# A two-layer trunk on one core: modulation scale on VectorE, low weight parts by adding transfers, one transfer rate in the planner, an earlier layer norm

## The chip, the core and the metric

The kernel runs on one core of a Trainium2 chip. A time is the device time of one execution in microseconds; the figure for a kernel is the median of several executions. The engines are named as in the profile: PE (TensorE, matmul) with PEld (its weight loads), DVE (VectorE), ACT (ScalarE), POOL (GpSimd) and SP (SyncE, whose queue carries most transfers).

## The reference: what is computed

Two layers run over 640 tokens (128 context tokens and 512 latent tokens) of width 1024. All is float32. Cut to what matters here:

```python
mod = silu(c) @ w_mod + b_mod              # six vectors a layer, for the context and for the latents
sh1, sc1, gt1, sh2, sc2, gt2 = split(mod, 6)
h = rmsnorm(x, g_pre_mix) * (1 + sc1) + sh1
bg, cg, xin, q, k, v, cf_u, ga, gb, gc = split_in(h @ w_in)      # 8704 columns
y_a = (bg * dwconv(cg * xin)) @ sc_w_out                         # width 3
y_b = diff_attention(q, k, v) @ attn_w_out                       # 8 heads, two maps each
z = dwconv(za * sigmoid(zg), cf_conv_w) + cf_conv_b              # width 31
y_c = silu(layernorm(z)) @ cf_w_out + cf_b_out
m = sigmoid(ga) * y_a + sigmoid(gb) * y_b + sigmoid(gc) * y_c
x = x + gt1 * rmsnorm(m @ w_o)
h = rmsnorm(x) * (1 + sc2) + sh2
x = x + gt2 * rmsnorm(square(relu(h @ w_ff1)) @ w_ff2)
```

## The kernel before

**Tiling.** Channels lie on the 128 partitions and the 640 tokens along the row, so x, h and every branch are 8 (or 4) tiles `u` of 128x640. A product is computed to nearly float32 with three fast matmuls: both operands are split into a high part, which the fast format holds exactly, and the rest. The tiles `h[k]` are such pairs.

**Weights.** `raw_load` brings a block of 128x1024 (512 KB) to one of three buffers `raw`, through SP's queue. `wblock` makes two of ten buffers `w` of it: `wh` is a cast on ACT, `wl = r - wh` a subtraction that the planner puts on DVE or on POOL (`nc.either`). A block serves 48 matmuls of 128x320. In the MLP `wseven` also knows another way to a low part for some of its seven operands: ACT writes `-r` to it (rounded as `wh` is), and a transfer issued from POOL reads the weight in memory again and adds it (`accum_op=ALU.add`).

**Order of the work.** The code is not issued as it is written. A `Recorder` collects operations with the tiles that they touch; `rank` gives each a due time (that of the matmul that needs it, less the durations on the way), and `schedule` plays the engines forward with modelled durations, picking what is due first, and sets each engine's order and what of `either` goes to POOL. In that model a transfer of SP's takes its bytes over 360 GB/s, one after another; a transfer of POOL's takes 3 us and its bytes over 150 GB/s, beside the others.

**Start.** The 8 tiles of x are loaded and squared, their mean square is summed over the channels on PE, and `rsb`, the reciprocal root for each token, is copied to all partitions. Then for each k of 8: x[k] is multiplied by `rsb`; the scale (j = 1) and the shift (j = 0) of block k are two products of a 128x1024 piece of `w_mod` with the two vectors `cc`: the piece comes as two tiles `u` of 128x512, and 8 matmuls with 2 columns (16 instructions in the profile, `ps<-cc,u`) give 2 columns of the PSUM tile `gp`, to which DVE adds the bias (`mod`). DVE makes `der` (gain times 1 + scale), ACT applies both (`u<-u,mod,der`), ACT and DVE split the result to `h[k]`, and `first_k` runs its matmuls: 12 of 128x256 (`pp<-u,w`) and 9 of 128x384 (`ps<-u,w`) for four blocks of `w_in`, the gates of the first two tiles of the long convolution; the fourth block's second part follows in `proj_half`. These are called the lead products here. All other modulation vectors are made later by `modvec`: a row-wise product of a raw tile with `cb` (c and c_ctx after silu, repeated on all partitions) and its sum on DVE, two of them for each tile (`junk<-raw,cb` and `raw<-raw,cb`). `cond` loads `cb`; it stands behind the lead loop.

**Attention part.** For each head `k_head` and `q_head` project, rotate (half of the rotation goes through 4 transfers `u<-u` inside SBUF) and split; `scores`, `softmax`, `values` and `v_pair` follow. `cgate` and `short` are the convolution branches; their taps run on DVE in between. `mt(i)` is a block of `w_in`.

**Gates.** `gated` runs three rounds of 8 tiles (A, B, C): the gate's product with h, a sigmoid, and the branch's product. `convnorm` is the layer norm of the long convolution in three steps (mean, variance, apply), one step with each of the tiles d = 5, 6, 7 of round A (`if d >= KD - 3: next(cn)`). Behind round A the heads' outputs `o` are loaded (`u<-on`, `u<-rqd`), scaled and split for round B.

Of the kernel before, what the change touches and what calls it, by code (L numbers as in the profile page):

```python
# [184 lines left out]


class Recorder:
# [132 lines left out]
    def rank(self):  # L320
# [18 lines left out]
        for op in reversed(self.ops):  # L339
            d = op.dur  # L340
            if op.eng == "sync":
                d = 1.3 + op.acts[1] / 360e3
            elif op.eng == "gpsimd" and op.acts is not None:
                d = 3.0 + op.acts[1] / 150e3
# [5 lines left out]
    def schedule(self):  # L350
# [91 lines left out]
        while len(seq) < n:  # L442
# [48 lines left out]
            if e == "sync":  # L491
                gen[0] = max(start, gen[0]) + 0.65
                dma[0] = max(gen[0] + 0.65, dma[0]) + op.acts[1] / 360e3
                op.end = dma[0]
            elif e == "gpsimd" and op.acts is not None:
                op.end = start + 3.0 + op.acts[1] / 150e3
            else:
                op.end = start + dur
# [34 lines left out]
def trunk_kernel(ctx: ExitStack, tc: tile.TileContext, xT, crow, ccol, wmod, wmod0, win, wv, wa, wc, wattn, wo, wff1, wff2,  # L533
# [68 lines left out]
    def wblock(src, eng=None):  # L602
# [3 lines left out]
        (eng or nc.either).tensor_sub(wl, r, f(wh))  # L606
# [288 lines left out]

    def modvec(l, st, j):
# [3 lines left out]
        for m in range(KD):  # L900
            r = raw_load(wmod[l, j * KD + m])
            for g in range(2):
                junk = r if g else wp.tile([P, KD * P], F32, tag="sum", name=nm("junk"), bufs=NSUM)
                nc.vector.tensor_tensor_reduce(out=junk, in0=r, in1=cb[:, g], op0=ALU.mult, op1=ALU.add, scale=1.0,
                                               scalar=0.0, accum_out=part[:, m, g:g + 1])
# [27 lines left out]
    nc.scalar.activation(cc, cc, AF.Silu)  # L933
    rsb = U()
# [5 lines left out]
    gp = PS()  # L940
    ts = [PP() for _ in range(2)]
# [9 lines left out]
    for k in range(KD):  # L951
        nc.either.tensor_mul(x[k], x[k], rsb)
        for j in (1, 0):
            i0 = j * KD + k
            r = half_tiles(wmod0[i0])
            sl = mod[:, i0, :]
            o = OFF["b_mod"][0] + i0
            nc.begin()
            for i in range(KD):
                c = (i % 4) * P  # L960
                nc.tensor.matmul(gp[:, 2 * i0:2 * i0 + 2], r[i // 4][:, c:c + P], cc[:, i, :], start=(i == 0),
                                 stop=(i == KD - 1))
            nc.done()
            nc.vector.tensor_scalar(sl, gp[:, 2 * i0:2 * i0 + 2], p[:, o:o + 1], None, op0=ALU.add)
# [9 lines left out]
    cond()  # L974
# [3 lines left out]
    for l in range(DEPTH):  # L978
# [3 lines left out]
        def mt(i):  # L982
            return wblock(win[l, i])
# [71 lines left out]
        def v_pair(pi):  # L1055
            wbs = [wblock(wv[l, 2 * pi + i]) for i in range(2)]
# [55 lines left out]
        def k_head(hd):  # L1112
# [3 lines left out]
            r = rope(proj2(wblock(win[l, W_K + hd]), h), kk, 1.0)  # L1116
# [9 lines left out]
        def q_head(hd):  # L1126

            r = rope(proj2(wblock(win[l, W_Q + hd]), h), None, QK ** -0.5)
# [186 lines left out]
        def gated(gate, n):  # L1315

            q = []
            for d in range(KD + n):
                if d < KD:
                    pg = proj(mt(gate + d), h)  # L1320
# [48 lines left out]
        for d, sg in gated(W_GA, 1):  # L1369
# [4 lines left out]
            if d >= KD - 3:  # L1374
# [245 lines left out]
def _layout(inp):  # L1620
# [8 lines left out]
    out["wmod0"] = _blocks(w0)  # L1629
# [71 lines left out]
```

## Time and profile before

| | |
|---|---|
| median of 3 runs (lowest, highest) | 2597.32 us (2591.19, 2600.37) |
| profiled execution: time, span | 2599.19 us, 2597.4 us |
| mean granted clock of TensorE | 0.972 |
| busy: PE, DVE, ACT, POOL | 96%, 74%, 48%, 11% |
| moved by the transfers | 336.76 MB, 130 GB/s over the span |

The profiled execution's time is 1.9 us above the median. Nearly all instructions carry one line of the code, that of the recorder's call, so groups are told apart by the names of the tiles: `out<-in`. The profile's rows of a timeline give start, duration, engine, operation, names, size and count, and in brackets the idle time before and what ended it. A table of windows gives the busy time of each engine in a stretch, the count of instructions, TensorE's granted clock as a share of full speed, the share of the transfer engines that was busy, and GB/s.

### The profile page before, as it was taken

What the parts mean: (1) busy time and instruction counts of PE and PEld (TensorE: products, weight loads), DVE (VectorE), ACT (ScalarE), POOL (GpSimd) and SP (SyncE); (2) the same over time, 40 slices, a digit from 0 to 9 for tenths busy, and PEclk for the clock granted to TensorE, in tenths of its full rate; (3) what the DMA queues carried; (4) which work ended last, traced back from release to release, by engine and by line L of the source; (5) the groups of instructions that cost most, each with busy time, mean ns of one, the idle gap of its engine ahead of it and who ended that gap; (6) DMA issues with size and microseconds to landing.
All of it is one profiled execution on the core that took longest, in us unless ns stands there. A gap on an engine that the chain in (4) does not pass through costs nothing.

```text
span 2597.4 us, 42157 instructions
## 1 busy us (share of the span) xinstructions
PE 2488.8 (96%) x16596; PEld 2412.5 (93%) x16596; DVE 1911.8 (74%) x3104; ACT 1250.4 (48%) x2323; POOL 290.7 (11%) x227
## 2 busy tenths in 40 slices
PE   7999999999999999999999999999999999999998
PEld 7988889999999899998988888999999999999998
DVE  3289786977785698878566887969566748677874
ACT  3365564223223566765445655532232247667653
POOL 1022110001020100012011211000011100001121
PEclk8899999999999999999989999999999999999999
DMA  7122222235554344577523222213454532447671
GB/s 269 48 93 65 66 68 71 87 127 194 176 178 138 99 166 175 191 176 187 171 87 97 76 62 77 73 56 115 154 174 137 175 110 96 140 156 210 176 216 56
DMA packets 132875, 336.76 MB, mean 130 GB/s; under 512 B 16244, under 2 KB 39108, under 8 KB 132676
## 3 DMA queue, kind: packets, MB, share of 16 engines
q1 hardware_dynamic: 122308, 315.19, 36.5%
q0 software_dynamic: 10368, 18.88, 4.3%
q8 instruction: 130, 2.13, 0.3%
q14 instruction: 69, 0.57, 0.1%
HBM read 284.15 MB, written 41.46 MB: 125 GB/s over the span
## 4 chain that ended last, share of the span: by engine, by line
PE 77%; DVE 11%; DMA 5%; ACT 4%; issue 2%; SPq 1%; POOL 0%; DVEq 0%; ACTq 0%; POOLq 0%
PE ps L529 41%; PE pp L529 35%; DVE u L529 8%; ACT u L529 3%; DMA raw<-in_wff_dram 2%; DMA u<-fd 2%; DVE w L529 1%; ACT w L529 1%; DVE mx L529 1%; DMA u<-u 1%; DVE sum L529 1%; SPq L529 1%; DMA u<-on 0%; DMA u<-rqd 0%; POOL st L529 0%
## 5 line engine op out<-in xcount | busy, mean ns | idle before, releaser
L529 PE MATMUL pp<-u,w 128*128 128x320 f32 (+1 forms) x6912 | 1069.6, 312 | 26.3 <-DVE u L529 12.9
L529 PE MATMUL ps<-u,w 128*128 128x320 f32 (+2 forms) x6672 | 1066.2, 315 | 12.1 <-DVE u L529 6.9
L529 PEld LDWEIGHTS pp<-u,w 128*128 128x128 f32 x6912 | 1030.1, 191 | 35.4 <-ACT u L529 13.6
L529 PEld LDWEIGHTS ps<-u,w 128*128 128x128 f32 x6672 | 1010.0, 191 | 25.0 <-DVE u L529 9.2
L529 ACT CAST w<-raw 128x1024 fp32r<-128x1024 f32 (+1 forms) x364 | 313.7, 863 | 290.2 <-PE ps L529 154.6
L529 DVE TENSOR_TENSOR w<-raw,w 128x1024 fp32r<-128x1024 f32 (+1 forms) x271 | 302.6, 1118 | 170.1 <-ACT w L529 166.7
L529 DVE TENSOR_TENSOR u<-u,u 128x640 fp32r<-128x640 f32 (+8 forms) x443 | 324.3, 744 | 72.8 <-ACT u L529 68.4
L529 ACT CAST u<-u 128x640 fp32r<-128x640 f32 (+2 forms) x280 | 195.5, 703 | 156.2 <-DVE u L529 79.7
L529 DVE SCALAR_TENSOR_TENSOR u<-u,par,u 128x640 f32<-128x640 f32 (+13 forms) x272 | 225.8, 863 | 1.7
L529 ACT ACTIVATE u<-u 128x320 f32<-128x320 f32 (+3 forms) x232 | 138.6, 612 | 117.8 <-DVE u L529 109.3
L529 DVE TENSOR_TENSOR w<-sum,w 128x512 fp32r<-128x512 f32 x208 | 143.4, 697 | 43.2 <-ACT w L529 42.2
L529 ACT CAST w<-sum 128x512 fp32r<-128x512 f32 x208 | 127.2, 621 | 87.2 <-PE pp L529 36.5
L529 ACT ACTIVATE u<-pp 128x640 f32<-128x640 f32 (+4 forms) x96 | 52.1, 552 | 234.1 <-PE pp L529 223.3
L529 POOL TENSOR_TENSOR u<-u,u 128x640 f32<-128x640 f32 (+4 forms) x60 | 104.6, 1747 | 503.2 <-DVE u L529 302.1
L529 DVE TENSOR_TENSOR u<-u,ps 128x320 f32<-128x320 f32 (+4 forms) x230 | 106.7, 481 | 52.8 <-PE ps L529 52.2
L529 DVE TENSOR_TENSOR u<-ps,u 128x512 fp32r<-128x512 f32 (+6 forms) x206 | 98.3, 505 | 59.8 <-PE ps L529 33.9
L529 DVE CUSTOM_DVE_ANT_0 junk<-raw,cb 128x1024 f32<-128x1024 f32 x80 | 102.5, 1283 | 46.7 <-DMA raw<-in_wmod_dram 46.5
L529 POOL DMA_DIRECT2D w<-in_wff_dram x72 | 62.9, 873 | 612.9 <-DVE sum L529 361.6
L529 PE MATMUL ps<-w,u 128*128 128x256 f32 x960 | 127.7, 291 | 2.8 <-ACT vo L529 2.8
L529 ACT ACTIVATE u<-pp,mx 128x640 f32<-128x640 f32 x128 | 101.0, 793 | 58.4 <-DVE mx L529 57.4
L529 PEld LDWEIGHTS ps<-w,u 128*128 128x128 f32 x960 | 120.9, 197 | 6.9 <-ACT vo L529 4.0
L529 POOL TENSOR_TENSOR w<-raw,w 128x1024 fp32r<-128x1024 f32 x21 | 52.9, 2521 | 565.6 <-ACT w L529 459.9
(90 smaller groups left out, 1874.5 us busy)
## 6 DMA issues: line engine op xcount, KB each, us to landing
raw<-in_wff_dram SPq DMA_DIRECT2D x128, 512.0 KB, 3.9
raw<-in_win_dram SPq DMA_DIRECT2D x120, 512.0 KB, 3.3
raw<-in_wmod_dram SPq DMA_DIRECT2D x80, 512.0 KB, 3.4
fd<-u SPq DMA_DIRECT2D x64, 320.0 KB, 2.4
u<-fd SPq DMA_DIRECT2D x64, 320.0 KB, 5.6
w<-in_wff_dram POOLq DMA_DIRECT2D x72, 256.0 KB, 5.8
u<-in_wmod_dram SPq DMA_DIRECT2D x32, 256.0 KB, 6.1
raw<-in_wv_dram SPq DMA_DIRECT2D x16, 512.0 KB, 3.3
```

What stands on the lines that cost most here:

```text
L529: getattr(eng, m)(*[r(v) for v in a], **{x: r(v) for x, v in k.items()})
```

## The change

1. **First scale on VectorE.** In the lead loop the shift (j = 0) stays on PE. The scale (j = 1) is made like the later modulation vectors: its piece of `w_mod` comes whole and with output channels on the partitions as a `raw` tile, two row-wise products with `cb` on DVE give `part[:, k]`, and DVE adds the bias. `cond` moves ahead of the loop.
2. **Low parts by adding transfers.** The blocks of `w_in` and of v's weights that pass through `mt` outside the gates, `v_pair`, `k_head` and `q_head` (40 a layer) get `wl` as in `wseven`: ACT writes `-r`, a POOL transfer adds the weight. The lead blocks and the gates' blocks keep the subtraction.
3. **Planner.** Transfers of SP and POOL share one modelled rate of 330 GB/s, an adding transfer counts twice its bytes, 0.7 to 1 us are added for landing, and the due times allow twice that duration.
4. **Layer norm one tile earlier.** `convnorm` takes its steps with d = 4, 5, 6.

```diff
+DMA = 330e3
...
             if op.eng == "sync":
-                d = 1.3 + op.acts[1] / 360e3
+                d = 2.0 + op.acts[1] / DMA / 0.5
             elif op.eng == "gpsimd" and op.acts is not None:
-                d = 3.0 + op.acts[1] / 150e3
+                d = 3.0 + 2 * op.acts[1] / DMA / 0.5
...
-                dma[0] = max(gen[0] + 0.65, dma[0]) + op.acts[1] / 360e3
-                op.end = dma[0]
+                dma[0] = max(gen[0] + 0.65, dma[0]) + op.acts[1] / DMA
+                op.end = dma[0] + 0.7
             elif e == "gpsimd" and op.acts is not None:
-                op.end = start + 3.0 + op.acts[1] / 150e3
+                dma[0] = max(start + 1.5, dma[0]) + 2 * op.acts[1] / DMA
+                op.end = dma[0] + 1.0
...
-    def wblock(src, eng=None):
+    def wblock(src, add=False):
         r = raw_load(src)
         wh, wl = wtile(), wtile()
         nc.scalar.copy(wh, r)
-        (eng or nc.either).tensor_sub(wl, r, f(wh))
+        if add:
+            nc.scalar.mul(wl, r, -1.0)
+            nc.gpsimd.dma_start(wl, src, accum_op=ALU.add)
+        else:
+            nc.either.tensor_sub(wl, r, f(wh))
         return wh, wl
...
+    def dots(r, out):
+        for g in range(2):
+            junk = r if g else wp.tile([P, KD * P], F32, tag="sum", name=nm("junk"), bufs=NSUM)
+            nc.vector.tensor_tensor_reduce(out=junk, in0=r, in1=cb[:, g], op0=ALU.mult, op1=ALU.add, scale=1.0,
+                                           scalar=0.0, accum_out=out[:, g:g + 1])
...
+    cond()
     rsb = U()
...
         for j in (1, 0):
             i0 = j * KD + k
-            r = half_tiles(wmod0[i0])
...
+            if j == 0:
+                r = half_tiles(wmod0[i0])
...
+            else:
+                r = raw_load(wmod0[i0])
+                dots(r, part[:, k])
+                nc.vector.tensor_scalar(sl, part[:, k], p[:, o:o + 1], None, op0=ALU.add)
...
-    cond()
...
         def mt(i):
-            return wblock(win[l, i])
+            return wblock(win[l, i], True)
...
-            wbs = [wblock(wv[l, 2 * pi + i]) for i in range(2)]
+            wbs = [wblock(wv[l, 2 * pi + i], True) for i in range(2)]
...
-            r = rope(proj2(wblock(win[l, W_K + hd]), h), kk, 1.0)
+            r = rope(proj2(wblock(win[l, W_K + hd], True), h), kk, 1.0)
...
-            r = rope(proj2(wblock(win[l, W_Q + hd]), h), None, QK ** -0.5)
+            r = rope(proj2(wblock(win[l, W_Q + hd], True), h), None, QK ** -0.5)
...
-                    pg = proj(mt(gate + d), h)
+                    pg = proj(wblock(win[l, gate + d]), h)
...
-            if d >= KD - 3:
+            if KD - 4 <= d < KD - 4 + 3:
                 next(cn)
...
-    out["wmod0"] = _blocks(w0)
+    out["wmod0"] = np.concatenate([_blocks(w0[:, :D]), w0[:, D:].T.reshape(KD, P, D)])
```

**What moves, engine by engine.** PE in the lead loop, before: the third block pair of k = 2 (`u_421` and `u_423` are `h[2]`, `ps_236` is `gp`, `w_198` to `w_254` are lead weights), between the shift's and the next scale's small products.

```order
L529 MATMUL ps_317<-u_421,w_207 128x384
L529 MATMUL ps_236<-cc_125,u_153 128x2 x4
L529 MATMUL ps_236<-cc_125,u_155 128x2 x4
L529 MATMUL ps_331<-u_421,w_234 128x384
L529 MATMUL ps_331<-u_423,w_234 128x384
L529 MATMUL ps_331<-u_421,w_246 128x384
L529 MATMUL ps_338<-u_421,w_249 128x384
L529 MATMUL ps_338<-u_423,w_249 128x384
L529 MATMUL ps_338<-u_421,w_254 128x384
L529 MATMUL ps_236<-cc_125,u_157 128x2 x4
L529 MATMUL ps_236<-cc_125,u_175 128x2 x4
L529 MATMUL pp_300<-u_480,w_198 128x256
```

The same engine and place now (`u_379` and `u_393` are `h[2]`, `u_429` and `u_443` are `h[3]`):

```order
L532 MATMUL ps_385<-u_379,w_158 128x384
L532 MATMUL ps_385<-u_393,w_158 128x384
L532 MATMUL ps_385<-u_379,w_160 128x384
L532 MATMUL ps_389<-u_379,w_188 128x384
L532 MATMUL ps_389<-u_393,w_188 128x384
L532 MATMUL ps_389<-u_379,w_192 128x384
L532 MATMUL pp_354<-u_429,w_162 128x256
L532 MATMUL pp_354<-u_443,w_162 128x256
```

No small product stands between k = 0 and k = 5 any more: those of six shifts are issued ahead of `h[0]`, those of the last two behind the first matmuls of k = 5 and ahead of k = 6.

DVE in the lead loop now, from the low part of `h[1]` (`u_361`) to that of `h[2]` (`u_393`); `raw_311` and `raw_319` hold the scale's pieces, the unnamed rows `part_291` read the sums:

```order
L532 TENSOR_TENSOR u_361<-u_338,u_352 128x640
L532 TENSOR_SCALAR der_316<-mod_240,par_130 128x2
L532 ISA raw_311,part_291<-raw_311,cb 128x1024
L532 ISA part_291 128x1
L532 ISA junk_381,part_291<-raw_319,cb 128x1024
L532 ISA part_291 128x1
L532 TENSOR_TENSOR u_393<-u_369,u_379 128x640
```

Before, only the split, `mod` and `der` stood there for each k; two row-wise products for each k have come between.

POOL at the start of the attention part, before (`w` is a low part by subtraction, `rp` is the rotation):

```order
L529 TENSOR_TENSOR w_995<-raw_785,w_974 128x1024
L529 TENSOR_TENSOR u_588<-u_988,u_979 128x512
L529 TENSOR_TENSOR u_1091<-u_1013,rp 128x512
L529 TENSOR_TENSOR u_1093<-u_1093,rp 128x512
L529 TENSOR_TENSOR vc_1162<-vo_1146,vc_1162 128x128
```

The same engine and place now:

```order
L532 DMA w_502<-in_win_dram 128x1024
L532 DMA w_627<-in_win_dram 128x1024
L532 DMA w_668<-in_win_dram 128x1024
L532 DMA w_680<-in_win_dram 128x1024
L532 DMA w_721<-in_wv_dram 128x1024
L532 DMA w_821<-in_wv_dram 128x1024
L532 DMA w_877<-in_win_dram 128x1024
L532 DMA w_933<-in_win_dram 128x1024
L532 TENSOR_TENSOR u_1041<-u_964,rp 128x512
```

Over the whole program POOL's subtractions `w<-raw,w` of 128x1024 go from 21 to 3 and DVE's from 187 to 125, POOL gains 80 transfers and ACT 80 products `w<-raw`; of the rotation's products `u<-u,rp` and sums of 128x512, 8 more stand on DVE and 8 fewer on POOL. On SP the MLP's transfers stand nearly as before; layer 1's loads `u<-on` and `u<-rqd` begin a few rows earlier, and the layer norm's stores `zd<-u`, which stood behind all but one of them, now stand among the later ones.

More of the change, by code (lines that the diff above doesn't have):

```diff
@@ L901, in modvec @@
             r = raw_load(wmod[l, j * KD + m])
[L902 to L905, printed above, removed]
+            dots(r, part[:, m])
             yield
@@ L940, in trunk_kernel @@
     gp = PS()
+    part = sm.tile([P, KD, 2], F32, tag="part", name=nm("part"), bufs=2)
     ts = [PP() for _ in range(2)]
@@ L954, in trunk_kernel @@
             i0 = j * KD + k
-            r = half_tiles(wmod0[i0])
             sl = mod[:, i0, :]
             o = OFF["b_mod"][0] + i0
[L958 to L964, printed above, removed]
+            if j == 0:
+                r = half_tiles(wmod0[i0])
+                nc.begin()
+                for i in range(KD):
+                    c = (i % 4) * P
+                    nc.tensor.matmul(gp[:, 2 * i0:2 * i0 + 2], r[i // 4][:, c:c + P], cc[:, i, :], start=(i == 0),
+                                     stop=(i == KD - 1))
+                nc.done()
+                nc.vector.tensor_scalar(sl, gp[:, 2 * i0:2 * i0 + 2], p[:, o:o + 1], None, op0=ALU.add)
+            else:
+                r = raw_load(wmod0[i0])
+                dots(r, part[:, k])
+                nc.vector.tensor_scalar(sl, part[:, k], p[:, o:o + 1], None, op0=ALU.add)
         o = OFF["g_pre_mix"][0] + k
```

## The prediction

> **What bounds the kernel now.** I read the page's busy line and its clock line, then the chain that ended last.
>
> ```profile
> PE 2488.8 (96%) x16596; PEld 2412.5 (93%) x16596; DVE 1911.8 (74%) x3104; ACT 1250.4 (48%) x2323; POOL 290.7 (11%) x227
> PEclk8899999999999999999989999999999999999999
> PE 77%; DVE 11%; DMA 5%; ACT 4%; issue 2%; SPq 1%; POOL 0%; DVEq 0%; ACTq 0%; POOLq 0%
> ```
>
> PE is the bound: it is idle for only 109 of 2597 us. Time can be won in two ways: from that idle time, or from stretches in which PE is busy at less than its full clock. The clock digits say where the second lies, so next I made windows of the start, and two short ones around a later change of clock. Behind the busy times of PE, PEld, DVE, ACT and POOL stand the granted clock, the transfer engines' share and GB/s.
>
> ```profile
> 20.00:40.00 20.00, 16.40 (x83) 15.94 (x84) 10.95 (x14) 5.70 (x8) 6.31 (x5) 1.00 1.04 394
> 39.00:107.00 68.00, 67.72 (x368) 67.11 (x368) 15.72 (x40) 22.25 (x35) 0.00 (x0) 0.67 0.14 48
> 50.00:65.00 15.00, 15.00 (x70) 15.00 (x70) 3.37 (x13) 4.12 (x7) 0.00 (x0) 0.52 0.02 6
> 213.00:217.00 4.00, 1.70 (x9) 0.98 (x7) 3.97 (x6) 2.08 (x6) 2.86 (x2) 1.00 0.12 33
> 217.00:221.00 4.00, 2.89 (x11) 2.70 (x12) 3.80 (x8) 2.04 (x4) 0.00 (x0) 0.60 0.37 131
> ```
>
> In the lead products (39 to 107 us) PE is never idle, but its clock is 0.67. DVE and POOL do almost nothing there, and the transfer engines are 14% busy. So this stretch pays for every PE instruction and for the clock, and for nothing else.
>
> **The change, term 1: the first scale on DVE.** The timeline of that stretch gives the prices (start, duration, engine).
>
> ```profile
> 32.83 0.58 PE L529 MATMUL pp<-u,w 128*128 128x256 f32 x1 [2.30 <-ACT u L529]
> 59.45 1.20 ACT L529 ACTIVATE u<-u,mod,der 128x512 f32<-128x512 f32 x2 [8.60 <-DVE mod L529]
> 61.03 3.41 PE L529 MATMUL ps<-cc,u 128*128 128x2 f32 x16
> 62.07 0.71 ACT L529 CAST u<-u 128x640 fp32r<-128x640 f32 x1
> 62.81 0.83 DVE L529 TENSOR_TENSOR u<-u,u 128x640 fp32r<-128x640 f32 x1 [0.27 <-ACT u L529]
> 64.73 0.23 DVE L529 TENSOR_SCALAR der<-mod,par 128x2 f32<-128x2 f32 x1
> 86.22 2.91 PE L529 MATMUL pp<-u,w 128*128 128x256 f32 x12
> 88.92 2.91 PE L529 MATMUL ps<-u,w 128*128 128x384 f32 x9
> 91.67 1.58 PE L529 MATMUL pp<-u,w 128*128 128x256 f32 x12
> 93.08 0.69 PE L529 MATMUL ps<-u,w 128*128 128x384 f32 x3
> 102.67 5.59 PE L529 MATMUL ps<-u,w 128*128 128x384 f32 x32
> ```
>
> One set of small products (16 instructions) costs 3.41 us at the low clock, and each k has two. The 21 lead matmuls of a k cost 2.91 + 2.91 = 5.8 us at the low clock. Where two k follow each other with no small products between (86 to 94 us) the same 12 fall from 2.91 to 1.58 us and the 9 to 3 x 0.69 = 2.07: 3.65 us for a k. So the small products cost twice: their own 3.41 us, and the clock of what follows them. The window of 50 to 65 says it most sharply: PE busy for 15.00 of 15.00 us, clock 0.52. The Trainium skill ("TensorE: Matmul & The Clock Gate", Part 1: The HAM clock gate) has a monitor that frees the clock after some 3.4 us of sustained activity. This window differs: the measurement decides, unless matmuls of 2 columns don't count as activity, which the page doesn't say. By the page's bare rule (busy is enough) it is not the small products that hold the clock down, and it would stay low without them; that is rival A's time.
>
> The change removes half of the small products, and most others move ahead of `h[0]`. What comes in on DVE, and what starts the stretch:
>
> ```profile
> L529 DVE CUSTOM_DVE_ANT_0 junk<-raw,cb 128x1024 f32<-128x1024 f32 x80 | 102.5, 1283 | 46.7 <-DMA raw<-in_wmod_dram 46.5
> 2.12 5.46 DMA u<-in_xT_dram
> ```
>
> Start: up to the first scale's tile SP's queue now has 8 tiles of x (320 KB each), 4 weight blocks and `cb` (6 x 512 KB), 12 half tiles of six shifts (256 KB each), the tile itself (512 KB) and some 1 MB of small constants: 10.5 MB. At the 394 GB/s of the window 20 to 40, from 2.1 us on, the tile lands at about 29 us. Two dots (2.6), `mod` and `der` (0.5), ACT 1.20 + 0.71 and, as my estimate, 3 us for landing and for the waits between five instructions put `h[0]` at about 37 us; before, the first matmul stood at 32.83. The start gets some 4 us later.
>
> Pace: per k DVE has two dots (2.57), the split (0.83), `mod` and `der` (0.46) and reading the sums (about 0.1, my estimate from the smallest row, 0.23): 4.0 us. PE needs 3.65 at the full clock. DVE paces, with PE 90% busy, in gaps of 0.35 us. So the last k is ready at 37 + 7 x 4.0 = 65; then 3.65 for it, 5.6 for the rest of the fourth block (the row at 102.67, whose 32 matmuls reach to 108) and about 1.8 for the last two shifts (1.7 each at the full clock, one of the two in PE's gaps): 76 instead of 108, -32 us. Behind it the first block with an adding transfer must wait for buffers `w` that the lead holds; ACT's write, POOL's issue and the landing (rows below: 1.0, 0.9, 5.8) take some 8 us from then, beside about 5 us of matmuls on blocks already made: +3. Term 1 is **-29**. Ends: with the clock low all the way 37 + 8 x 5.8 + 2 x 3.41 + 32 x 2.91/9 = 100.6, which is -7; at PE's pace, from 36 on, 36 + 8 x 3.65 + 5.6 = 71, which is -37. I take a value near the full clock because of 86 to 94 us: two k without small products are enough there.
>
> **Term 2: adding transfers in the attention parts.** Windows of both layers, the groups concerned (busy and mean ns; idle before), waits of PE, and the transfers (KB, us to landing):
>
> ```profile
> 107.00:465.00 358.00, 340.32 (x2294) 311.07 (x2293) 288.39 (x479) 195.66 (x409) 50.05 (x34) 0.98 0.24 77
> 1395.00:1731.00 336.00, 316.67 (x2129) 287.14 (x2128) 276.95 (x459) 184.29 (x391) 49.67 (x34) 0.98 0.22 70
> L529 DVE TENSOR_TENSOR w<-raw,w 128x1024 fp32r<-128x1024 f32 x187 | 245.0, 1311 | 143.5 <-ACT w L529 140.1 <-PE ps L529 2.6 <-issue 0.3
> L529 POOL TENSOR_TENSOR w<-raw,w 128x1024 fp32r<-128x1024 f32 x21 | 52.9, 2521 | 565.6 <-ACT w L529 459.9 <-DMA u<-rqd 105.6
> 22.14 2.55 DVE L529 TENSOR_TENSOR w<-raw,w 128x1024 fp32r<-128x1024 f32 x1
> L529 ACT CAST w<-raw 128x1024 fp32r<-128x1024 f32 x208 | 217.7, 1048 | 247.7 <-PE ps L529 137.7 <-PE pp L529 82.7 <-issue 10.3
> L529 POOL DMA_DIRECT2D w<-in_wff_dram x72 | 62.9, 873 | 612.9 <-DVE sum L529 361.6 <-ACT w L529 191.8 <-DVE u L529 36.7
> PE ps L529 <- DVE u L529: 9.9, 8, 2.8
> PE ps L529 <- DVE u L529: 10.2, 9, 2.8
> q0 software_dynamic: 10368, 18.88, 4.3%
> w<-in_wff_dram POOLq DMA_DIRECT2D x72, 256.0 KB, 5.8
> u<-u SPq DMA_DIRECT2D x128, 64.0 KB, 2.0
> by line: PE ps L529 58.1%; DVE u L529 12.1%; PE pp L529 7.0%; ACT u L529 5.1%; issue 3.3%; DVE mx L529 3.1%; DMA u<-u 3.1%; SPq L529 2.1%; DVE w L529 1.4%; DMA raw<-in_wv_dram 0.9%; ACT w L529 0.8%; DVE pc L529 0.7%; DVE su L529 0.6%; POOL
> ```
>
> Gain. 62 subtractions leave DVE (62 x 1.31 = 81 us of its 565 in both windows) and 18 leave POOL (18 x 2.52 = 45 us, during which a DVE operation with two inputs can double: 2.55 at 22.14 beside one of POOL's, mean 1.31). Eight products and sums of the rotation come to DVE, some 10 us. PE is idle for 18 + 19 = 37 us in these stretches, and waits for DVE's `u` for 9.9 + 10.2 = 20 us of it. That is the ceiling, -20; the floor is 0, since the waits may come from the length of the chain of a head (rotate, split, softmax) instead of a full DVE. DVE is 81% busy there, so both count: I take half, -10.
>
> Costs. ACT's 80 products at about 1.05 us (the cast of the same size) lie on an engine that is 55% busy: nothing, else at most what ACT's share of the chain says. POOL's 80 issues at 0.87 replace 45 us of subtraction. The transfers: 4.3% of 2597 us over 72 is 1.55 us of all 16 engines for 256 KB, so 3.1 us for 512 KB, 248 us over the 694 us of both windows, 35% of the time. Ahead of PE stand the swaps `u<-u` of the rotation: 3.1% of this chain's 360 us is 11 us, with the other layer about 20, so about 10 of the 32 swaps (2 us each) lie on the path. Each met by a whole transfer: 10 x 0.35 x 3.1 = +11; by none, 0. The transfer engines are 24% busy and serve several queues at once, so I take +2. Term 2 is **-8**, between -20 and +11.
>
> **Term 3: the layer norm one tile earlier.** The window of its end and PE's waits in it:
>
> ```profile
> 603.00:634.00 31.00, 26.17 (x185) 25.42 (x184) 28.66 (x44) 17.77 (x24) 8.27 (x4) 1.00 0.77 249
> 612.67 1.11 PE L529 MATMUL pp<-u,w 128*128 128x320 f32 x6 [1.04 <-DVE u L529]
> 618.11 1.60 PE L529 MATMUL ps<-ident,st 128*128 128x128 f32 x12 [1.46 <-POOL st L529]
> 633.48 8.71 PE L529 MATMUL pp<-u,w 128*128 128x320 f32 x47 [2.32 <-ACT u L529]
> ```
>
> The three waits make 4.8 us, about as much in layer 2. With 5 us more of PE's work behind the mean and the variance, the second can go; the third waits for ACT, whose row of activations stays as long. I take 4 of 9 to 10: **-4**, between 0 and -8.
>
> **Term 4: the planner's rate.** The MLP's transfers on SP keep their order, and in the whole trace PE waits little for adding transfers:
>
> ```profile
> PE pp L529 <- DMA w<-in_wff_dram: 3.2, 2, 1.6
> ```
>
> I take 0, between -4 and +4.
>
> **Sum.** -29 - 8 - 4 = -41 on the profiled execution's 2599.2 (2597.4 of span and 1.8 around it) is 2558; the median is 1.9 below that execution, so **2556 us**.
>
> **Rivals.**
> A, the clock stays low in the lead products. For: it is low there now with PE full. Against: 86 to 94 us. Term 1 is -7, the sum -19: 2578.
> B, the adding transfers meet the swaps, and DVE's relief brings nothing: term 2 is +11 and the sum -22, 2575. For: 35% of the time has such a transfer. Against: the transfer engines' 24%.
> C, slower than before: every swap waits behind a whole adding transfer. There are 32 (128 transfers, 4 each), 32 x 3.1 = +99 against -33 of the other terms: 2663. It decides once a swap loses more than 33/32 = 1.03 us in the mean. Against: in the MLP transfers from SP land in a few us beside POOL's.
> D, the additions land late and PE waits for weights. In the MLP 72 of 256 KB cost PE 3.2 us; 80 of twice the size at twice the price each are +7: 2563. The gain is gone at 41/80 = 0.5 us each. For: behind ACT's write an addition needs 0.9 to be issued and over 5.8 to land. Against: ten buffers `w` hold five blocks, 48 matmuls each. The Trainium skill speaks against the change here ("SBUF — State Buffer", SBUF: two separate sides): a transfer issued from POOL writes its descriptors through a port that some DVE instructions lock, so that it starts late beside a busy DVE. If each were late by one DVE instruction of 1.3 us with no cover, that would be 104 us; the 3.2 us above, beside a DVE that works in the MLP too, speak against it.
>
> **How the numbers follow.** Forecast 0.62, A 0.16, B 0.11, C 0.05, D 0.06. The forecast's own span is 2538 to 2570; with A, B and D the range is 2536 to 2582, which leaves C and the outer parts of A and B out. A difference below 0.3% (8 us) can't be told from none. Faster: the forecast and D, and most of A and B, 0.88; same: the weak ends of A and B, 0.06; slower: C and a little beside it, 0.06.
>
> **What would show it.** Right: PE's clock near 1 from about 40 to 75 us with DVE about full there, the first K head some 30 us earlier, fewer subtractions on DVE and fewer waits of PE for DVE's `u` in the attention parts. Wrong: matmuls of 2.91 us for 12 in the lead (A); swaps well over 2.0 us and more `DMA u<-u` on the chain (B, C); PE waiting for `w<-in_win_dram` (D). The prediction fails most easily if DVE's pace in the lead is well above 4 us a k: each 0.5 us there costs 4.

## The result and the profile after

| | before | after |
|---|---|---|
| median, 4 runs each | 2598.85 us | 2536.76 us (2532.35 to 2539.58) |
| ratio of the times, 95% interval | | 0.9762 (0.9743 to 0.9781) |
| profiled execution: time, span | 2599.19, 2597.4 us | 2537.56, 2535.7 us |
| mean granted clock of TensorE | 0.972 | 0.984 |

The kernel is 2.4% faster: 62 us, where 41 were forecast (2556 us, range 2536 to 2582). The sign is right, and the time lies inside the range, 0.8 us above its lower end. Which terms were mis-sized is read first from where in the run the time was won, and then from runs of the single parts.

First the same lines of the page as before: busy engines, clock, and the chain that ended last.

```profile
PE 2444.4 (96%) x16468; PEld 2372.8 (94%) x16468; DVE 1844.3 (73%) x3084; ACT 1321.6 (52%) x2403; POOL 303.0 (12%) x279
PEclk9999999999999899999989999999999998999999
PE 80%; DVE 5%; issue 5%; ACT 4%; DMA 4%; POOL 1%; SPq 1%; DVEq 0%; ACTq 0%; POOLq 0%
```

PE has 128 instructions less, all of them small products, and 44 us less busy time; its idle time fell from 108.6 to 91.3 us. On the chain DVE's share halved, from 11% to 5%.

**The two traces laid over each other.** All kernels of this study issue the same lead, projection, attention and MLP matmuls. So I count PE's instructions in windows of 5 us and ask at which time equally many are left. The difference is the lead that a kernel has over the kernel before at that point of the work. The first column is the time in the kernel before (us); the other columns are leads in us (negative: ahead). They come from one profiled execution each, and a few us of them differ from run to run. A matmul that reaches from one window into the next is counted in both; counted by their starts alone, single entries move by up to 3 us. The profiled executions of edits 1 and 4 alone lie 6 and 7 us below the medians of their kernels, so these two columns end lower than the medians do.

| before, at | stage that ends there | after | 1 scale | 2 adds | 3 planner | 4 norm | without 3 | without 4 | without 2 |
|---|---|---|---|---|---|---|---|---|---|
| 238 | start, lead, first heads | -27.1 | -29.1 | 2.7 | 1.7 | -3.7 | -25.5 | -28.7 | -31.5 |
| 527 | attention, layer 1 | -27.6 | -30.7 | 5.7 | 8.6 | -3.8 | -22.4 | -31.4 | -19.2 |
| 595 | gates A | -27.7 | -30.3 | 5.8 | 9.0 | -3.6 | -22.3 | -31.1 | -19.2 |
| 670 | layer norm | -34.4 | -29.7 | 7.3 | 15.7 | -6.7 | -23.6 | -26.6 | -25.7 |
| 1093 | gates, first MLP part | -36.1 | -29.7 | 8.9 | 15.6 | -7.3 | -23.8 | -26.8 | -25.5 |
| 1249 | second MLP part | -44.9 | -33.8 | 8.1 | 6.1 | -10.8 | -25.2 | -36.7 | -36.0 |
| 1766 | attention, layer 2 | -47.3 | -39.3 | 6.8 | 4.6 | -16.6 | -22.1 | -44.7 | -39.1 |
| 1834 | gates A | -47.0 | -38.8 | 6.9 | 5.0 | -16.5 | -21.5 | -44.3 | -38.8 |
| 1909 | layer norm | -53.2 | -37.9 | 4.6 | 10.7 | -19.6 | -25.4 | -38.6 | -45.5 |
| 2329 | gates, first MLP part | -51.7 | -36.0 | 6.0 | 11.7 | -19.0 | -22.2 | -36.5 | -44.4 |
| 2482 | second MLP part | -63.1 | -34.9 | 6.5 | 1.9 | -18.8 | -23.8 | -44.6 | -53.3 |

Read down the column "after": 27 us are won at the start, nothing in layer 1's attention, 6 to 7 at each layer norm, 9 to 11 in each second MLP part, and 2 net from 1249 to 1766. The forecast had put 29 at the start, 8 in the attention of both layers together, 4 at the two norms together, and nothing in the MLP.

**The start.** Windows and PE's timeline of the changed kernel:

```profile
39.00:75.00 36.00, 31.73 (x201) 31.26 (x201) 26.38 (x66) 18.39 (x28) 1.06 (x1) 1.00 0.53 165
50.00:65.00 15.00, 15.00 (x96) 15.00 (x96) 15.00 (x33) 9.52 (x14) 0.76 (x1) 1.00 0.44 143
37.14 3.57 PE L532 MATMUL ps<-cc,u 128*128 128x2 f32 x16 [0.31 <-DVE mod L532]
42.11 3.58 PE L532 MATMUL ps<-cc,u 128*128 128x2 f32 x16 [1.40 <-DVE mod L532]
45.95 0.58 PE L532 MATMUL pp<-u,w 128*128 128x256 f32 x1 [0.26 <-ACT u L532]
49.15 2.72 PE L532 MATMUL pp<-u,w 128*128 128x256 f32 x11 [2.62 <-DVE u L532]
54.19 1.57 PE L532 MATMUL pp<-u,w 128*128 128x256 f32 x12
55.60 1.73 PE L532 MATMUL ps<-u,w 128*128 128x384 f32 x9
57.17 1.57 PE L532 MATMUL pp<-u,w 128*128 128x256 f32 x12
66.48 1.84 PE L532 MATMUL ps<-cc,u 128*128 128x2 f32 x16
78.06 12.22 PE L532 MATMUL ps<-u,w 128*128 128x384 f32 x77
```

The window of 50 to 65 us stood at a clock of 0.52 before and has 1.00 now, and the lead matmuls of a k take 3.0 us from start to start (54.19 to 57.17; the durations of its two rows overlap). At the low clock they took 5.5 (86.22 to 91.67 in the kernel before), and two sets of small products came on top. But the first lead matmul waits until 46 us, and the second until 49. DVE's own rows say why:

```profile
36.87 0.22 DVE L532 TENSOR_SCALAR mod<-ps,par 128x2 f32<-128x2 f32 x1 [2.20 <-PE ps L532]
38.13 1.22 DVE L532 CUSTOM_DVE_ANT_0 junk<-raw,cb 128x1024 f32<-128x1024 f32 x1
```

The first dots stand behind the bias of a shift that waits for PE's small products. (The clock column shows 1.00 from the first window on, but the trace holds no record of the clock before 53.7 us, 36.9 in the kernel before, and the column counts such time as full. That the matmuls before then still run at half speed is read from their durations: 2.72 us for 11 and 3.57 for 16, against 1.57 for 12 and 1.84 for 16 later.)

**Attention.** PE's waits for DVE and for ACT in layer 1 (110 to 455 us) and layer 2 (1340 to 1670) of the changed kernel, then the row for ACT's `pc` in layer 1 of the kernel before and of the run without edit 2 that follows below (us in total, times, longest), then the chain through layer 1, the queue of the adding transfers, ACT's new group, and the transfers' landing:

```profile
PE ps L532 <- DVE u L532: 3.6, 9, 1.1
PE pp L532 <- ACT pc L532: 6.8, 4, 3.1
PE ps L532 <- DVE u L532: 4.0, 7, 1.3
PE pp L532 <- ACT pc L532: 8.2, 5, 2.7
PE pp L529 <- ACT pc L529: 1.3, 3, 0.6
PE pp L533 <- ACT pc L533: 2.5, 2, 1.6
by line: PE ps L532 56.0%; ACT u L532 9.1%; DMA u<-u 7.2%; PE pp L532 6.6%; DVE u L532 6.3%; issue 4.8%; SPq L532 2.1%; DMA raw<-in_wv_dram 1.7%; DVE mx L532 1.5%; DMA out_dram<-vo 1.1%; ACT w L532 1.1%; ACT pc L532 0.7%; POOL rq L532 0.5%; 
q0 software_dynamic: 21888, 60.83, 14.1%
L532 ACT ACTIVATE w<-raw 128x1024 fp32r<-128x1024 f32 x80 | 85.0, 1063 | 78.3 <-PE ps L532 76.1 <-PE pp L532 2.1
w<-in_win_dram POOLq DMA_DIRECT2D x64, 512.0 KB, 5.7
w<-in_wv_dram POOLq DMA_DIRECT2D x16, 512.0 KB, 7.9
u<-u SPq DMA_DIRECT2D x128, 64.0 KB, 2.3
```

The relief came: PE's waits for DVE's `u` fell from 9.9 and 10.2 to 3.6 and 4.0 us. A new wait took its place: PE waits 6.8 and 8.2 us for ACT's `pc` (1.3 and 3.1 before, 2.5 in either layer without edit 2), while ACT has 85 us more to do, the 80 low parts. On layer 1's chain the swaps `u<-u` went from 3.1% to 7.2%, 11 to 26 us. Their median landing hides why. Over the swaps' transfers whose landing can be told in the trace (101 of 128 before, 100 after), the mean went from 2.10 to 3.09 us, and 26 took more than 4 us, where none had; without edit 2 the mean is 2.13. So the gain turned into waits for ACT and for transfers, and both come with the adding transfers. How much is ACT's work and how much the transfers' isn't separated by a run.

### The profile page after: what moved, and what is told of

The parts are those of the page before. It is cut to its first block, busy times and chain, and to the rows that moved or that the text cites. A ratio compares the mean times of both kernels' runs of the same rounds, so it can differ in the third digit from the quotient of the medians.

```text
span 2535.7 us, 42084 instructions
## 1 busy us (share of the span) xinstructions
PE 2444.4 (96%) x16468; PEld 2372.8 (94%) x16468; DVE 1844.3 (73%) x3084; ACT 1321.6 (52%) x2403; POOL 303.0 (12%) x279
## 3 DMA queue, kind: packets, MB, share of 16 engines
q1 hardware_dynamic: 121156, 315.19, 36.9%
q0 software_dynamic: 21888, 60.83, 14.1%
## 4 chain that ended last, share of the span: by engine, by line
PE 80%; DVE 5%; issue 5%; ACT 4%; DMA 4%; POOL 1%; SPq 1%; DVEq 0%; ACTq 0%; POOLq 0%
PE ps L532 42%; PE pp L532 38%; DVE u L532 4%; ACT u L532 3%; DMA u<-u 2%; SPq L532 1%; DMA w<-in_wff_dram 1%; POOL w L532 1%; ACT w L532 0%; DVE mx L532 0%; DVE w L532 0%; DMA raw<-in_win_dram 0%; POOL st L532 0%; ACT pc L532 0%; DMA raw<-in_wv_dram 0%
## 5 line engine op out<-in xcount | busy, mean ns | idle before, releaser
L532 PE MATMUL pp<-u,w 128*128 128x320 f32 (+1 forms) x6912 | 1052.8, 309 | 13.2 <-DVE u L532 9.1
L532 PEld LDWEIGHTS pp<-u,w 128*128 128x128 f32 x6912 | 1017.0, 189 | 17.7 <-DVE u L532 12.1
L532 PEld LDWEIGHTS ps<-u,w 128*128 128x128 f32 x6672 | 1005.3, 190 | 17.7 <-issue 7.5
L532 DVE TENSOR_TENSOR u<-u,u 128x640 fp32r<-128x640 f32 (+8 forms) x450 | 318.9, 721 | 60.2 <-ACT u L532 56.2
L532 DVE TENSOR_TENSOR w<-raw,w 128x1024 fp32r<-128x1024 f32 (+1 forms) x209 | 222.6, 1066 | 148.4 <-ACT w L532 144.5
L532 DVE SCALAR_TENSOR_TENSOR u<-u,par,u 128x640 f32<-128x640 f32 (+15 forms) x272 | 221.6, 849 | 5.6 <-ACT u L532 3.3
L532 ACT ACTIVATE w<-raw 128x1024 fp32r<-128x1024 f32 (+1 forms) x152 | 130.5, 859 | 104.5 <-PE ps L532 82.6
L532 DVE CUSTOM_DVE_ANT_0 junk<-raw,cb 128x1024 f32<-128x1024 f32 x88 | 116.9, 1329 | 36.7 <-DMA raw<-in_wmod_dram 36.6
L532 POOL TENSOR_TENSOR u<-u,u 128x640 f32<-128x640 f32 (+3 forms) x53 | 98.4, 1862 | 366.6 <-DVE u L532 303.7
```

The source lines that it names most:

```text
L532: getattr(eng, m)(*[r(v) for v in a], **{x: r(v) for x, v in k.items()})
```

## The experiments

Each kernel was timed against the kernel before on the same chip; ratios are given with their 95% interval. Not all kernels ran on one chip. Where two of them are held against each other below, the distance is that of their medians, and by their ratios it is up to 4 us other (35 for 37, 25 for 22, 8 for 5, 6 for 8, 46 for 44). The first four make one edit alone.

**Edit 1 alone.** The scale's dots, `cond` ahead of the loop, the rest as before:

```diff
+    cond()
...
+                r = raw_load(wmod0[i0])
+                dots(r, part[:, k])
```

> Only the first scale on VectorE (and cb ahead of the loop), the rest as before. In the two traces the same matmul of PE stands 27 us earlier at 217 us into the changed kernel than in the kernel before. Theory: that whole lead is this edit's and is kept to the end: -22 to -30 us, clock 1.00 in the lead products. Rival: part of the lead comes from the planner's rate, which orders the start's transfers and PE's small products too: then -10 to -18.

Measured 2569.47 us, ratio 0.9901 (0.9876 to 0.9927): -26 us. Its lead at 238 us is -29.1, within the noise as large as that of the whole change. So the gain at the start is this edit's, and the rates have no part in it that shows.

**Edit 2 alone.**

```diff
-        (eng or nc.either).tensor_sub(wl, r, f(wh))
+        if add:
+            nc.scalar.mul(wl, r, -1.0)
+            nc.gpsimd.dma_start(wl, src, accum_op=ALU.add)
```

> Only the adding transfers for the low parts, with the planner's rates of before (3 us and 150 GB/s for a transfer of POOL's). Over layer 1's attention the lead of the changed kernel doesn't grow (-27.1 to -27.4 us), over layer 2's it grows by about 6. Theory: relief of VectorE and late additions nearly cancel: 0 to -6 us. Rival: the planner of before takes an addition to land within 6.5 us beside all other transfers, places them too late, and PE waits for w<-in_win_dram: +5 to +30 us, so that the planner's edit is what makes this one bearable.

Measured 2604.51 us, ratio 1.0042 (1.0024 to 1.0060): slower by 11 us. The rival named the right sign and size, but PE waited for `w<-in_win_dram` in no row; the loss is 3 us at the start and 3 in layer 1's attention in its column, and little after it. There (110 to 455 us) PE's waits for DVE's `u` fell from 9.0 to 3.0 us, and those for ACT's `pc` and `u` rose from 1.3 and 2.8 to 6.9 and 5.9.

**Edit 3 alone.**

```diff
+DMA = 330e3
...
-                d = 1.3 + op.acts[1] / 360e3
+                d = 2.0 + op.acts[1] / DMA / 0.5
```

> Only the planner's rates. Between 1060 and 1190 us and between 2270 and 2460 us of the changed kernel (end of the attention half and the MLP, where no other edit stands) the lead grows by some 8 and 10 us, PE's waits for VectorE's u falling from 8.4 to 3.4 and from 7.6 to 3.2 us. Theory: the rates do this, so alone they give -10 to -18 us. Rival: those stretches gain because the order there shifts by chance with what stands ahead of them: alone 0, between -5 and +5.

Measured 2597.13 us, ratio 1.0009 (0.9994 to 1.0023): no change. Neither expectation holds as it was put. The column shows why: 9.5 and 9.8 us are won in the second MLP parts as the theory says, and 7 lost in layer 1's attention, 7 and 6 at the layer norms. A sum of nothing hid two effects of opposite sign. At layer 1's norm PE's wait for ACT is 9.12 us, where it was 2.32:

```profile
647.79 12.41 PE L533 MATMUL pp<-u,w 128*128 128x320 f32 x65 [9.12 <-ACT u L533]
```

**Edit 4 alone.**

```diff
-            if d >= KD - 3:
+            if KD - 4 <= d < KD - 4 + 3:
```

> Only the layer norm one tile earlier. The lead grows by 6.5 us at layer 1's norm and by 6 at layer 2's, and PE is idle for 4.9 and 3.5 us less there. Theory: this edit removes all of PE's waits around the norm, and the clock that they cost: -10 to -13 us. Rival, as I forecast: the last wait, for ScalarE, stays or moves to the next consumer: -4 us, and the rest of the 12 comes from the earlier loads of o, which the planner's edit moved.

Measured 2587.39 us, ratio 0.9973 (0.9956 to 0.9990): -7 us, between the two. One wait is left at the norm of layer 1 (2.25 us for POOL's `st`), and the lead grows by 3 us at each norm.

By their ratios the four alone make -26 + 11 + 2 - 7 = -20 us; together they make -62. So two or more of them must act on each other. The next runs leave one out.

**All without edit 3.** (diff against the changed kernel)

```diff
-                d = 2.0 + op.acts[1] / DMA / 0.5
+                d = 1.3 + op.acts[1] / 360e3
...
-                op.end = dma[0] + 0.7
+                op.end = dma[0]
```

> The changed kernel with the planner's rates of before (edits 1, 2 and 4 stay). Theory: the rates are worth some 10 to 18 us here: 2547 to 2555. Rival: they are worth nothing by themselves: 2533 to 2541. A third way: without them the additions land late, and it is over 2565.

Measured 2573.80 us, ratio 0.9896 (0.9873 to 0.9919): the size of the third way, but not its cause, since PE waits for `w<-in_win_dram` in no row here either. It is 37 us slower than the changed kernel, and about the sum of edits 1, 2 and 4 alone (-22). The column stays between -21 and -26 from layer 1's attention to the end: against the changed kernel 17 us are missing in the two second MLP parts, 8 at the norms, 4 in layer 1's attention and 5 between 1249 and 1766. Edit 3, worth nothing alone, carries 37 us here.

**All without edit 4.**

```diff
-            if KD - 4 <= d < KD - 4 + 3:
+            if d >= KD - 3:
```

> The changed kernel with the layer norm's steps where they were (edits 1, 2 and 3 stay). Alone, the norm's edit gave -7 us and the planner's +2. With the planner's rates alone PE waits 9.1 us for ScalarE's u behind layer 1's norm, where it waited 2.3 before, and the run falls 7 us back there. Theory: the planner's rates cost the norm some 10 us a layer, and the earlier norm takes that back: without it 2555 to 2565. Rival: the two only add: about 2544.

Measured 2558.96 us, ratio 0.9860 (0.9835 to 0.9884): 22 us slower than the changed kernel, as the theory said, against 7 us that the norm's edit gave alone. At the two norms it falls back by 4.5 and 5.7 us where the changed kernel gains 6.7 and 6.2. DVE's order shows the mechanism. Here are the statistics of the norm (`st`, 128x5) and the first of the subtractions that follow from it (`u<-u,ps` 128x320) in the kernel before, then the same two and PE's wait in this one:

```profile
616.09 0.15 DVE L529 TENSOR_SCALAR st<-ps 128x5 f32<-128x5 f32 x1
622.12 0.48 DVE L529 TENSOR_TENSOR u<-u,ps 128x320 f32<-128x320 f32 x1
586.27 0.16 DVE L533 TENSOR_SCALAR st<-ps 128x5 f32<-128x5 f32 x1
600.87 1.27 DVE L533 TENSOR_TENSOR u<-u,ps 128x320 f32<-128x320 f32 x3
609.39 10.84 PE L533 MATMUL pp<-u,w 128*128 128x320 f32 x61 [7.17 <-ACT u L533]
```

6.0 us lie between them before, 14.6 with the planner's rates: more of the scaling of the heads' outputs (`u<-u,gsub,u`), dots of the later modulation and the low part of a weight have come between, ACT's activations come later by as much, and PE waits 7.17 us. With the norm one tile earlier the same order costs nothing, since PE has another tile's gates to do:

```profile
567.00:600.00 33.00, 33.00 (x236) 32.87 (x235) 31.86 (x49) 18.32 (x22) 4.29 (x2) 1.00 0.75 257
```

PE is busy for 33.00 of 33 us there.

**All without edit 2.**

```diff
-            nc.scalar.mul(wl, r, -1.0)
-            nc.gpsimd.dma_start(wl, src, accum_op=ALU.add)
+            nc.either.tensor_sub(wl, r, f(wh))
```

> The changed kernel without the adding transfers (edits 1, 3 and 4 stay; low parts by subtraction). The adding transfers alone gave +11 us. Theory: with the planner's rates the additions are placed where they land in time, and are worth 0 to -10 us: 2537 to 2547 here. Rival: they cost here too, and the gain beyond the sum of the parts is the planner's with the norm's alone: 2522 to 2532, a kernel faster than the changed one.

Measured 2541.98 us, ratio 0.9794 (0.9773 to 0.9815): 5 us slower than the changed kernel; the intervals overlap. The theory's range held. The rates cost layer 1's attention 12 us when low parts are subtracted (-31.5 to -19.2), and nothing when they are added (-27.1 to -27.6): there the two edits help each other, though by less than the norm and the rates do.

**The clock.** One set of small products, then two, were put behind the lead products of each k. They read `h[k]` and write columns of `gp` that nobody reads; a third kernel has wide matmuls there.

```diff
             first_k(lead[hf], wbs, h, hf, k)
+        nc.begin()
+        for i in range(KD):
+            nc.tensor.matmul(gp[:, 64 + 2 * k:66 + 2 * k], f(h[k][0])[:, (i % 5) * P:(i % 5 + 1) * P], cc[:, i, :],
+                             start=(i == 0), stop=(i == KD - 1))
+        nc.done()
```

> The changed kernel with 8 small products (2 columns, 16 instructions) set behind the lead products of each k, which read h[k] and write columns of gp that nobody reads. Theory: small products cost twice, their time and the clock of the matmuls after them: the clock in the lead falls to 0.5 to 0.7 and a k goes from 3.3 to about 5.8 + 3.4 us, so +35 to +48 us. Rival: only their own time at the full clock counts, 8 x 1.8: +12 to +16 us, clock near 1.

> The control: the same place in each k, but 9 matmuls of 384 columns of the lead's own kind (about 1.7 us by the rows of the changed kernel) in place of the small products. Both theories: +12 to +16 us, clock 1.00. If the clock falls here too, it is not the two columns that hold it down.

```diff
+            nc.tensor.matmul(gp[:, 128:512], h[k][0][:, (i % 5) * P:(i % 5 + 1) * P], h[k][1][:, :384],
+                             start=(i == 0), stop=(i == 8))
```

Measured 2539.87 us with one set, ratio 0.9778 (0.9749 to 0.9807), and 2541.53 with the wide ones, 0.9784 (0.9755 to 0.9813). My theory fell in this form: with one set the clock stays at 1.00 and a set costs 1.84 us, as the rival said. The stretch of 60 to 75 us with one set:

```profile
60.00:75.00 15.00, 15.00 (x119) 15.00 (x118) 6.58 (x17) 5.23 (x8) 1.05 (x1) 1.00 0.59 175
62.46 1.84 PE L532 MATMUL ps<-cc,u 128*128 128x2 f32 x16
64.16 1.67 PE L532 MATMUL pp<-u,w 128*128 128x256 f32 x12
```

Either kernel ends its lead products about 14 us later than the changed one (8 sets of 1.8), but the whole run is only 3 to 5 us longer, inside the intervals. At 238 us it stands at -16.5 for -27.1, at 1397 at -39.5 for -45.4, at the end, by the spans, at -59.8 for -61.7. So not all of a gain at the start need be kept. That the engines that feed PE catch up while PE is late is how I read these columns; no run shows which of them does.

**Two sets for each k**, the share of before:

```diff
+        for c in (64, 96):
+            nc.begin()
+            for i in range(KD):
+                nc.tensor.matmul(gp[:, c + 2 * k:c + 2 + 2 * k], f(h[k][0])[:, (i % 5) * P:(i % 5 + 1) * P], cc[:, i, :],
```

> The changed kernel with two sets of small products (32 instructions, written to columns that nobody reads) behind the lead products of each k: some 3.6 us of every 6.9 at the full clock, 52% of PE's time, as before the change; with one set it was 35%, and the clock stayed at 1.00. Theory, mended: the clock falls once small products take about half of the time, so here it falls to 0.5 to 0.7, a k takes up to 12.6 us, and the lead products end 50 to 75 us later than in the changed kernel. Rival: small products don't hold the clock down at all, and the low clock before had another cause: 8 x 3.6 = 29 us later, clock 1.00.

```profile
65.00:100.00 35.00, 35.00 (x219) 35.00 (x219) 1.52 (x5) 1.93 (x3) 0.00 (x0) 0.74 0.20 53
100.00:115.00 15.00, 15.00 (x79) 15.00 (x80) 1.04 (x2) 3.36 (x5) 0.08 (x1) 0.61 0.00 1
82.01 4.69 PE L532 MATMUL ps<-cc,u 128*128 128x2 f32 x32
86.56 2.91 PE L532 MATMUL pp<-u,w 128*128 128x256 f32 x12
```

Measured 2581.03 us, ratio 0.9938 (0.9915 to 0.9961): 44 us slower than the changed kernel. PE is busy all the time and the clock falls to 0.74 and 0.61; 12 matmuls take 2.91 us again. The lead products end at 115 where they ended at 78: 37 us, between the two expectations, of which 8 x 3.6 = 29 are the products' own time. So the mended theory holds in kind and was too high in size: small products do hold the clock down with PE never idle, but only when they take about half of the time (52% at the full clock, 3.6 of every 6.9 us), not at 35%. By the Trainium skill ("TensorE: Matmul & The Clock Gate", Part 1: The HAM clock gate) the clock is freed after one busy window of about 3.4 us. Here 35 busy us in a row have a mean of 0.74, so the measurement decides against busy time as the measure. What in the small matmuls isn't counted was not tried. Nor is their share parted from the length of an unbroken row of them, except that the one row of 32 in the kernel with one set (3.63 us from 78.60) left the clock at 1.00.

**The late start.** The step of the forecast that was furthest off was the first lead matmul: 46 to 49 us for 37. Two kernels tried its cause. In the first the shift's bias goes to ACT; in the second the small products of k = 2 to 7 are also held back in the planner until `h[k-2]` is there:

```diff
-                nc.vector.tensor_scalar(sl, gp[:, 2 * i0:2 * i0 + 2], p[:, o:o + 1], None, op0=ALU.add)
+                nc.scalar.activation(sl, gp[:, 2 * i0:2 * i0 + 2], AF.Identity, bias=p[:, o:o + 1], scale=1.0)
```

> The changed kernel with the shift's bias added on ScalarE in place of VectorE. In the changed kernel the first lead matmuls stand at 46 to 49 us, where I forecast 37: on VectorE the first dots (38.1 us) stand behind the bias of the third shift (36.9), which waits for PE's small products. Theory: without that the dots start near 33 us and the low part of h[0] is there by 43; then the five sets of small products ahead of it on PE (3.58 us each from 26) are what ends last, at about 44: 3 to 5 us won at the start, 2530 to 2536 if they are kept. Rival: the scale's transfer lands late, and the first lead matmul stays at 46 or later: 2536 to 2540.

```diff
                 nc.begin()
+                if k > 1:
+                    nc.access(nc.group, h[k - 2][1], False)
```

> As bias_act, and the small products of the shifts of k = 2 to 7 are held back until h[k-2] is there, so that two sets stand ahead of the first lead matmuls and one set in each later k. Theory: PE starts the lead products at 39 to 41 us, the clock stays at 1.00 as with one added set for each k (35% of the time), each set costs 1.8 us in place of 3.58, and the lead products end 3 to 6 us earlier than in the changed kernel: 2529 to 2535. Rival: with small products between the first k the clock isn't freed, a k takes 9 us, and the lead products end 10 to 25 us later: 2545 to 2560.

```profile
40.63 3.57 PE L532 MATMUL ps<-cc,u 128*128 128x2 f32 x16 [0.35 <-ACT mod L532]
44.07 2.91 PE L532 MATMUL pp<-u,w 128*128 128x256 f32 x12
42.33 0.58 PE L532 MATMUL pp<-u,w 128*128 128x256 f32 x1 [13.20 <-ACT u L532]
49.19 1.84 PE L532 MATMUL ps<-cc,u 128*128 128x2 f32 x16
```

The first two rows are the bias on ACT, the last two the held sets. With the bias on ACT the dots start earlier, PE's small products end at 44.07 and the lead products follow with no gap, as expected: 2528.41 us, ratio 0.9738 (0.9714 to 0.9762). That is 8 us below the changed kernel and the fastest median here, but the intervals overlap. With the sets held back PE starts at 42.33, and the clock is freed all the same, each set at 1.84 us: 2533.54 us, 0.9763 (0.9739 to 0.9786), the same as the changed kernel. Now PE has idled for 13.2 us ahead of it, waiting for ACT's `u`, and does the sets' work later. So it was DVE's queue first and PE's queue of small products next; behind both stands the scale's own way through DVE and ACT, which ends at 42, not 37.

## Why the prediction was right, and where its sizes were wrong

- **The whole.** 62 us were won for 41 forecast. The direction and the largest term are right. The rest is not: attention gave next to nothing of its 8 us, the norms gave 13 for 4, and the second MLP parts, where nothing was forecast, gave 20. The forecast's own span ended at 2538; the range went 2 us lower, to 2536, without a term or a rival that gives such a time, and the measured 2536.76 fell into these 2 us. That was luck.
- **Term 1, the start: -29 forecast, -27 to -29 measured** (the traces at 238 us, edit 1 alone -26 in the median). Its inner steps were off in both directions. The lead products start at 46 to 49 us, not 37: I had counted the bytes to the scale's transfer, but not that its dots stand on DVE behind a bias that waits for PE's small products. The pace is 3.0 us for a k, not 4.0: DVE had worked ahead while PE was late, so PE, not DVE, set it. (My 3.65 for PE added two durations that overlap.) That the two errors cancel is luck.
- **The clock.** That small products cost twice holds, with a condition that I had missed: it needs about half of PE's time in them. Between 0 and 238 us the changed kernel spends 5 us more idle and 24 us less on the low clock (the sum of one minus the clock over the windows); 8 us are left of the -27. They are the difference of two things: eight sets less, 14.7 us at 1.84 each, and some 6 us, by subtraction, of matmuls at half speed ahead of the first clock record, which comes later here (53.7 us for 36.9) and which the column doesn't count. Rival A did not come.
- **Term 2, attention: -8 forecast, 0 in layer 1 and 2 net from the second MLP part to the end of attention in layer 2.** The relief of DVE is there (waits of 20.1 us to 7.6), but I priced ACT's 80 products at nothing because ACT was 55% busy. With them PE's waits for ACT's `pc` rose: 1.3 to 6.8 us in layer 1, 3.1 to 8.2 in layer 2, and 2.5 in either without the edit. The transfers' price was right: q0's share gives (14.1% of 2535.7 - 4.3% of 2597.4)/80 = 3.07 us each, where I had 3.1. What they do to the swaps was not: I put +2 us on it, and on layer 1's chain alone the swaps grew by 15 us. So rival B's mechanism came in good part. Its +11 for this edit is what the edit costs alone; with the other edits in place it is worth some 5 us.
- **Rivals C and D.** Neither time came. But the sign that I had named for C did: it was to decide once a swap loses more than 1.03 us in the mean. From the issue of a swap's first transfer to the last landing known of its four, the mean went from 3.9 to 5.5 us, 1.6 us more, and the kernel is faster all the same. So the threshold was wrong: it let the loss of all 32 swaps reach PE, where term 2 had about 10 of them on the path. For D: PE waits for no adding transfer of `w_in`. By the Trainium skill ("SBUF — State Buffer", SBUF: two separate sides) an issue on POOL can be held up beside a busy DVE. Here it takes no longer than in the MLP:

```profile
L532 POOL DMA_DIRECT2D w<-in_win_dram x64 | 56.7, 886 | 443.0 <-ACT w L532 378.2 <-ACT u L532 36.1 <-PE ps L532 28.3
```

  886 ns for 873. The blocks of `w_in` land in 5.7 us, 512 KB where 256 KB took 5.8; those of v's weights take 7.9. A delay that the MLP's transfers have as well would not show in this comparison.
- **Term 3, the layer norm: -4 forecast, -13 over the two norms in the traces, and 22 us in the run without it.** The step that failed is that the third wait, ACT's, would stay. All three waits went: in layer 1's stage of 595 to 670 us PE was idle for 4.8 us, and in the changed kernel (567.3 to 635.6) for none. And I had priced the edit against the waits of before, while the planner's edit in the same change would have made these waits three to four times as long (7.17 and 9.12 us for 2.32).
- **Term 4, the rates: 0 forecast, 37 us in the run without them.** I had looked at PE's waits for adding transfers alone and found 3.2 us. The page of before had the row that I passed over: `u<-fd`, the loads of the spilled MLP activations, with 2% of the chain. Here is that row, then DVE's and ACT's waits for these loads in the kernel before, with the rates alone, in the changed kernel and without the rates:

```profile
PE ps L529 41%; PE pp L529 35%; DVE u L529 8%; ACT u L529 3%; DMA raw<-in_wff_dram 2%; DMA u<-fd 2%; DVE w L529 1%; ACT w L529 1%; DVE mx L529 1%; DMA u<-u 1%; DVE sum L529 1%; SPq L529 1%; DMA u<-on 0%; DMA u<-rqd 0%; POOL st L529 0%
DVE u L529 <- DMA u<-fd: 11.2, 8, 3.6
ACT u L529 <- DMA u<-fd: 25.1, 25, 3.9
DVE u L533 <- DMA u<-fd: 2.6, 10, 0.4
ACT u L533 <- DMA u<-fd: 18.7, 14, 3.6
DVE u L532 <- DMA u<-fd: 0.2, 1, 0.2
ACT u L532 <- DMA u<-fd: 11.5, 10, 3.0
DVE u L529 <- DMA u<-fd: 11.3, 8, 3.3
ACT u L529 <- DMA u<-fd: 22.6, 22, 3.6
```

  Behind one such load stands PE's longest wait of this part in the kernel before:

```profile
1155.21 0.49 DVE L529 TENSOR_TENSOR u<-u 128x320 f32<-128x320 f32 x1 [3.61 <-DMA u<-fd]
1156.50 0.90 PE L529 MATMUL ps<-u,w 128*128 128x320 f32 x2 [3.08 <-DVE u L529]
```

  In every kernel with the new rates the second MLP parts win 8 to 11 us each, and in every kernel without them 4 at most. PE's idle time there is 10.2 and 9.5 us before, 4.4 and 2.8 in the changed kernel, and 9.7 in the first of the two parts without the rates. That the loads' earlier place is the whole cause there isn't shown by a run of its own; the waits and the leads agree in all kernels.

## What to carry to other kernels

Where a planner sets the order, an edit need not have a price of its own. The rates were worth nothing alone and some 35 us with the other edits, because what they lose at the layer norms and in layer 1's attention is what two other edits take away; so edits that move the same queue are forecast and tried together, and each left out once. When a change alters the rule that orders transfers, price every transfer that the chain of before names, however small its share, not only those that the change speaks of. And before an engine's spare time is taken as cover, look for what that engine does just ahead of the bound one: ACT was 55% busy, and PE's new waits for it are nearly as long as those for DVE that went. And read a transfer's mean landing beside its median: the swaps' median rose by 0.3 us, their mean by 1.0.

## What was not expected of the hardware

- PE's clock isn't held up by being busy: with PE never idle it was 0.52 before and 0.74 in the experiment with small products in about half of the time, and 1.00 with them in a third.
- Nor do small products alone free it. From 26 to 46 us of the changed kernel PE is busy for 17.7 of 20 us with them, and a set takes 3.4 to 3.6 us throughout, where it takes 1.84 later; the clock is on record as full from 53.7 us, 4.6 us after the lead matmuls begin to run without a gap (49.15).
- The clock column reads 1.00 in the first 50 us of the changed kernel although matmuls run at half of their later speed there, since the trace has no clock record that early; at the start of a program the durations say it, not the column.
